# Offsets between the moving and the stationary tiles of TensorE, set stage by stage

## The chip, the cores and the metric

The kernel runs on one core of a Trainium2 chip. The time is that of one execution on the device, in microseconds. Besides plain timed runs there is one profiled execution, whose trace is read here: it lists each instruction of TensorE (PE, with its weight loads as PEld), VectorE (DVE), ScalarE (ACT), GpSimd (POOL) and the DMA queues with start and end.

## The reference

A small network on 256 tokens of width 1024, all in float32. The first block is stick-breaking attention, a squared-ReLU MLP, retention and a second MLP. The second block is a hybrid mixer (gated delta rule and forgetting attention beside each other), then a layer of 16384 experts from which each head picks 16 by product keys:

```python
for layer in range(DEPTH):                       # first_block
    hn = rms_norm(h, g_mix[layer])
    h = h + (stick_breaking_attention(...) if layer % 2 == 0 else retention(...))
    h = h + squared_relu_mlp(rms_norm(h, g_mlp[layer]), w_mlp_up[layer], w_mlp_down[layer])
...
res = res + hybrid_mixer(rms_norm_2(res, norm_mix), ...)      # second_block
# peer_ffn: scores, top-k, softmax gate, then
act = gelu(einsum('thkd,td->thk', expert_u[idx], xb))
out = einsum('thk,thkd->td', gate_w * act, expert_v[idx])
```

## The kernel before

All products with weights are made in three passes of the format fp32r: each float32 operand is split into a high part and the rest (ScalarE copies the high part, VectorE subtracts: lines 277 and 278 for weights, 150 and 151 for activations), and `mm3` (lines 84 to 91) issues high by high (L88), high by rest (L89), rest by high (L91). Each of these matmuls has a stationary operand of 128 columns, which a LDWEIGHTS brings into the array, and a moving operand of 256 columns that streams through it. While one matmul streams, the weights of the next one are loaded. So two operands are read from SBUF at the same time: the moving tile of this matmul and the stationary tile of the next.

Weights come through `Weights`: SP's queue loads a raw tile of 128x1024 floats some tiles ahead (line 247), and the split halves stand in tiles `whi` and `wlo` of fixed size, so that their start within a partition, counted modulo 512 bytes, is the same for all. Activations (`nh`/`nl` before a layer, `uh`/`ul` in the MLP, `yh`/`yl` before an output projection, `br..` in the hybrid's branches) stand in tiles whose rows are 1024 bytes long. Where they start is set by small unused tiles that `shift(pool, n)` allocates ahead of them (n bytes, lines 153 to 155), and, for `nh`/`nl`, by the argument of `norm_begin` (an offset in bytes within a larger tile, lines 158 to 168). Where the weights are the moving operand (token-major projections `pv`, list `moving` of `weight_plan`), `split` places them at an offset within a larger tile (line 251, in elements).

The stages, in order, with the name of the PSUM tile of each product: attention (`pq`, `pk`, `pv`, `pout`, until about 125 us of the profile), MLP 0 (`pu` up, `pd` down, until 300), retention (`pqk`, `pv`, `pg`, `pout`, until 497), MLP 1 (`pu` until 585, `pd` until 675), the hybrid (until 1034, with its output branches `py` and `pout` until 1101), and the expert layer `peer`: queries `pq`, top-16 choice on VectorE and the experts' up products `ph` beside each other (until 1323), the table of gates G built with float32 matmuls `pg` between `ph` products (until 1582), and the down products `acc`. In those the weights are the moving operand, 512 columns wide, and the stationary operand is a 128-column piece of `ch` or `cl`, the split product of activation and gate (lines 1586 to 1599). The loads of the next weights and of the spilled activations run beside this on the DMA queues.

In the built program before, the start of the moving tile minus the start of the stationary tile that is loaded beside it is 192 modulo 512 bytes in every one of these stages, except in the hybrid's input projections, where the rows of the moving tile are 1088 bytes long, so that the distance takes all multiples of 64 in turn (and, for the 260 columns of its `pq`, 48 more than these).

Of the kernel before, what the change touches and what calls it, by code (L numbers as in the profile page):

```python
# [9 lines left out]
F32R = mybir.dt.float32r  # L10
# [8 lines left out]
T = 256  # L19
# [202 lines left out]
class Weights:  # L222
# [18 lines left out]
    def prefetch(self, i, raws=None, parts=None):  # L241

        raws = min(i + 2 * self.bufs if raws is None else raws, len(self.plan))
        parts = min(i + self.bufs if parts is None else parts, len(self.plan))
        while len(self.raw) < raws:
            raw = self.wp.tile([128, 1024], F32, tag="raw", name="raw", bufs=self.bufs + 1)
            self.nc.sync.dma_start(raw, self.plan[len(self.raw)])
            self.raw.append(raw)
        while len(self.parts) < parts:
            i = len(self.parts)  # L250
            self.parts.append(self.split(self.raw[i], 96 if i in self.moving else 0))

    def first_half(self, i):

# [32 lines left out]
def sb_layer(k, h, next_gain):  # L287

    nc, a = k.nc, k.a
    x = (klist(k.nh), klist(k.nl))  # L290
    st = {}
    with k.tc.tile_pool(name="sb", bufs=2) as sp:
# [91 lines left out]
        def main():  # L384
            yield from project_qk(0)
            for g in range(1, 4):
                yield from project_qk(g)
                yield from project_v(g - 1)
            yield from project_v(3)
            k.norm_begin(256)  # L390

            for b in (0, 2):
                ps = [k.lin([128, 2, T], "pout") for _ in range(2)]
                for i in range(2):
                    for j in range(2):
                        yield from k.proj_half(ps[j], a["w_sb_out"][b + j][i], i, xo)
                        yield
                for j in range(2):
                    m = 2 * (b + j)
                    nc.vector.tensor_tensor(h[:, m:m + 2, :], ps[j], h[:, m:m + 2, :], op=OP.add)  # L400
                    for i in range(2):
                        k.norm_tile(h, m + i, next_gain)
# [18 lines left out]
def mlp_layer(k, h, layer, after):  # L421
    nc, a = k.nc, k.a
    x = (klist(k.nh), klist(k.nl))
    with k.tc.tile_pool(name="mlp", bufs=2) as mp:
        k.shift(mp, 96 if layer else 192)
        uh = mp.tile([128, 32, T], F32R, name="uh", bufs=1)
        ul = mp.tile([128, 32, T], F32R, name="ul", bufs=1)
        for b in range(16):
            p = k.proj(a["w_mlp_up"][16 * layer + b], x, "pu")
            r = mp.tile([128, 2, T], F32, name="r")  # L430
            nc.scalar.activation(r, p, AF.Relu)
            sq = mp.tile([128, 2, T], F32, name="usq")
            nc.scalar.activation(sq, r, AF.Square)
            k.split(uh[:, 2 * b:2 * b + 2, :], ul[:, 2 * b:2 * b + 2, :], sq)
            if b == 0:
                rs = k.rstd_bc(k.ssq, T, "rstd")
                r2 = mp.tile([128, T], F32, name="rstd2", bufs=1)
                nc.vector.tensor_tensor(r2, rs, rs, op=OP.mult)
        xu = (klist(uh), klist(ul))
        after("begin")  # L440
        for m in range(8):
            p = k.proj_deep([a["w_mlp_down"][(8 * layer + m) * 4 + i] for i in range(4)], xu, "pd")
            d = mp.tile([128, T], F32, name="d")
            nc.vector.tensor_tensor(d, p, r2, op=OP.mult)
            nc.vector.tensor_tensor(h[:, m, :], d, h[:, m, :], op=OP.add)
            after(m)


def ret_layer(k, h, next_gain):
    nc, a = k.nc, k.a  # L450
    x = (klist(k.nh), klist(k.nl))
    with k.tc.tile_pool(name="ret", bufs=2) as rp:
        k.shift(rp, 192)
        yh = rp.tile([128, 16, T], F32R, name="yh", bufs=1)
        yl = rp.tile([128, 16, T], F32R, name="yl", bufs=1)
        cs = rp.tile([128, 2, T], F32, name="cs", bufs=1)
# [3 lines left out]
        r = None  # L460
        for hd in range(4):
            rot = []
            for i in range(2):
                p = k.proj(a["w_ret_in"][4 * i + hd], x, "pqk")
# [18 lines left out]
            for b in range(2):  # L483
# [10 lines left out]
                p = drain(steps)  # L494
# [32 lines left out]
            for b in range(2):  # L527
# [1 line left out]
                nc.vector.tensor_tensor(yy, yy, gts[b], op=OP.mult)  # L529
                t0 = 4 * hd + 2 * b  # L530
                k.split(yh[:, t0:t0 + 2, :], yl[:, t0:t0 + 2, :], yy)
        k.norm_begin(256)
        xy = (klist(yh), klist(yl))
        for m in range(8):
            p = k.proj_deep([a["w_ret_out"][2 * m + i] for i in range(2)], xy, "pout")
# [13 lines left out]
class Hybrid:  # L549
# [749 lines left out]
    def branches(self, next_gain, get_ready):  # L1299

        k, nc, a = self.k, self.k.nc, self.k.a
        with k.tc.tile_pool(name="hbr", bufs=2) as bp:
            k.shift(bp, 96)

            xn = (klist(k.nh), klist(k.nl))
            yh = bp.tile([128, 8, T], F32R, name="yh", bufs=1)
            yl = bp.tile([128, 8, T], F32R, name="yl", bufs=1)
            gates = {bi: bp.tile([128, 2, T], F32, name=f"gate{n}", bufs=1) for n, bi in enumerate(gate_order()[:6])}
            pieces = {i: [tuple(bp.tile([128, T], F32R, name=f"br{z}{i}{m}", bufs=1) for m in range(8)) for z in "hl"]
                      for i in range(2)}  # L1310
            for n, bi in enumerate(gate_order()):
                if n < 6:
                    nc.scalar.dma_start(gates[bi], self.spill[n])
                else:
                    gates[bi] = bp.tile([128, 2, T], F32, name=f"gate{n}", bufs=1)

            def parts(i):
                for m in range(8):
                    k.split(pieces[i][0][m], pieces[i][1][m], (self.ob if i else self.oa)[:, m, :])
                return pieces[i]  # L1320

            for b, i in gate_order()[6:]:
                self.gate(gates[b, i], k.proj(a["w_hyb"][28 + 4 * i + b], xn, "pg"))
            x = {}
            for b in range(4):
                for i in (1, 0):
                    gt = gates[b, i]
                    if i not in x:
                        x[i] = parts(i)
                    p = k.proj(a["w_branch"][4 * i + b], x[i], "py")  # L1330
                    nc.vector.scalar_tensor_tensor(gt, gt, 1.0, p, op0=OP.add, op1=OP.mult)
                y = gates[b, 1]
                nc.vector.tensor_tensor(y, y, gates[b, 0], op=OP.add)
                hi = yh[:, 2 * b:2 * b + 2, :]
                nc.scalar.activation(hi, y, AF.Copy, scale=0.5)
                nc.vector.scalar_tensor_tensor(yl[:, 2 * b:2 * b + 2, :], y, 0.5, hi.bitcast(F32), op0=OP.mult,
                                               op1=OP.subtract)
            get_ready()
            xy = (klist(yh), klist(yl))
            for b in range(4):  # L1340
                p = k.proj(a["w_hyb_out"][b], xy, "pout")
                if b:
                    k.ahead.prefetch(0, parts=b - 1)
                hh = self.h[:, 2 * b:2 * b + 2, :]
                nc.vector.tensor_tensor(hh, p, hh, op=OP.add)
                for m in range(2):
                    k.norm_tile(self.h, 2 * b + m, next_gain)
# [33 lines left out]
def peer(k, h, gi, scoring):  # L1381
# [3 lines left out]
    with ExitStack() as ctx:  # L1385
        pp = ctx.enter_context(tc.tile_pool(name="peer", bufs=1))
        up = ctx.enter_context(tc.tile_pool(name="up", bufs=2))
        k.shift(up, 320)
        dr = ctx.enter_context(tc.tile_pool(name="spill", bufs=1, space=bass.MemoryType.DRAM))
        cols = pp.tile([128, 3, T], F32, name="cols")  # L1390
        iota = pp.tile([128, 128], F32, name="iota")
        nc.gpsimd.iota(iota, pattern=[[1, 128]], base=0, channel_multiplier=0, allow_small_or_imprecise_dtypes=True)
        spill = dr.tile([64, 128, 2, T], F32, name="spill")
        nh, nl = k.nh, k.nl
        r = k.rstd_bc(k.ssq, T, "rstd", pool=pp)
        rc = k.col(r, "rcol")
        xh = k.operand(k.act, "nh", T, 256)
        xl = k.operand(k.act, "nl", T, 256)
        x = (klist(xh), klist(xl))

        def normed(i):
# [169 lines left out]
        with tc.tile_pool(name="ops", bufs=1, space=PSUM) as ops:  # L1571
# [8 lines left out]
            for n, j in enumerate(down_order()):  # L1580
# [4 lines left out]
                    nc.scalar.dma_start(act, spill[j // 2])  # L1585
                c = up.tile([128, 2, T], F32, tag="t1", name="c")
                nc.vector.tensor_tensor(c, act, G[:, j:j + 2, :], op=OP.mult)
                ch = up.tile([128, 2, T], F32R, tag="t2", name="ch")
                cl = up.tile([128, 2, T], F32R, tag="t3", name="cl")
                k.split(ch, cl, c)  # L1590
                ws = [k.load_w(a["expert_v"][j + i]) for i in range(2)] if n == 63 else None
                c0, c1 = ([[z[:, i, 128 * t:128 * t + 128] for t in range(2)] for i in range(2)] for z in (ch, cl))
# [60 lines left out]
def body(tc, a, stop=None, start=None):  # L1653
    nc = tc.nc
    with ExitStack() as ctx:
# [11 lines left out]
        def after_gain(gi):  # L1667
            def f(m):
                if m == "begin":
                    k.norm_begin(256)  # L1670
                else:
                    k.norm_tile(h, m, gi)
            return f
# [3 lines left out]
        def get_ready():  # L1677

            k.shift(ctx.enter_context(tc.tile_pool(name="end", bufs=1, side="right")), 32)
            k.ahead = Weights(tc, ctx, peer_plan(a), 2, halves=True, side="right", name="wpp")  # L1680
            k.ahead.prefetch(0, parts=0)
            k.shift(c2.enter_context(tc.tile_pool(name="gap", bufs=1, side="right")), 320)
            k.norm_begin(0, c2.enter_context(tc.tile_pool(name="pnorm", bufs=1, side="right")))

        if start == "peer":
# [4 lines left out]
        else:  # L1690
            with ExitStack() as c1:
                plan, moving = weight_plan(a)
                k.w = Weights(tc, c1, plan, 3, moving=moving)
                with tc.tile_pool(name="attp", bufs=1, space=PSUM) as k.attp:
                    k.norm_begin(256)
                    splits = []
                    for i in range(2):
                        load_stream((i,))
# [121 lines left out]
```

## Time and profile before

| | us |
|---|---|
| median of 3 runs | 1948.25 (1946.83 to 1958.43) |
| profiled execution, its own time | 1947.31 |
| its span, first to last instruction | 1945.6 |
| PE busy / DVE busy / ACT busy | 1924.5 / 1426.5 / 1119.8 |

Of the profiled execution 1.7 us lie outside the span. A matmul's record lasts longer than the step from one matmul's start to the next, because matmuls are pipelined. What a stretch costs is therefore its length divided by the matmuls that start in it, and not the mean duration of one.

### The profile page before, as it was taken

How to read it: one execution, taken by the hardware profiler on the slowest of the kernel's cores; microseconds unless marked ns; L12 is line 12 of the kernel's file. 1: busy time of each engine (PE TensorE's matmuls, PEld its weight loads, DVE VectorE, ACT ScalarE, POOL GpSimd, SP SyncE). 2: the span in 40 equal slices, each digit the busy share in tenths (PEclk: the TensorE clock that was granted, in tenths of full speed). 3: DMA queues.
4: the chain of work that ended last, by engine and by line, in shares of the span. 5: the costliest groups of instructions: out<-in, count | busy, mean ns of one | idle time of the engine just before them, and what ended most of it. 6: DMA issues, size and time to landing. Idle time of an engine off the chain costs nothing.

```text
span 1945.6 us, 38035 instructions
## 1 busy us (share of the span) xinstructions
PE 1924.5 (99%) x14787; PEld 1819.0 (93%) x14787; DVE 1426.5 (73%) x2840; ACT 1119.8 (58%) x1761; POOL 118.7 (6%) x187
## 2 busy tenths in 40 slices
PE   8999999999999999999999999999999999999999
PEld 7999999999999988999899999999999998888887
DVE  5575556766655598688776799998888867777775
ACT  7776545556664475545555565446666655555554
POOL 2110000000000100110100111110000000000000
PEclk9999999999999999999999999999999999999999
DMA  6456666555666553332256357776555567777775
GB/s 196 141 164 194 196 195 191 166 177 174 207 192 192 174 168 98 98 99 77 88 188 219 125 179 226 222 226 189 179 179 176 180 206 235 235 236 234 236 234 179
DMA packets 109413, 353.63 MB, mean 182 GB/s; under 512 B 12832, under 2 KB 15664, under 8 KB 109104
## 3 DMA queue, kind: packets, MB, share of 16 engines
q1 hardware_dynamic: 97104, 329.82, 54.1%
q10 hardware_dynamic: 12128, 21.38, 3.4%
q8 instruction: 116, 1.90, 0.4%
q14 instruction: 65, 0.53, 0.1%
HBM read 332.28 MB, written 18.87 MB: 180 GB/s over the span
## 4 chain that ended last, share of the span: by engine, by line
PE 90%; DVE 6%; issue 3%; ACT 1%; POOL 0%; DMA 0%; SPq 0%; DVEq 0%; POOLq 0%; ACTq 0%
PE acc L1597 6%; PE acc L1596 6%; PE acc L1599 6%; PE ph L91 6%; PE ph L88 6%; PE ph L89 6%; PE pd L88 3%; PE pd L91 3%; PE pd L89 3%; PE pu L89 3%; PE pg L1565 3%; PE pu L91 3%; PE pu L88 3%; DVE wlo L278 2%; PE pv L88 1%
## 5 line engine op out<-in xcount | busy, mean ns | idle before, releaser
L278 DVE TENSOR_TENSOR wlo<-raw,whi 128x512 fp32r<-128x512 f32 (+1 forms) x863 | 774.4, 901 | 341.9 <-ACT whi L277 291.8
L277 ACT ACTIVATE whi<-raw 128x512 fp32r<-128x512 f32 (+1 forms) x863 | 675.1, 788 | 601.4 <-PE acc L1597 158.0
L88 PE MATMUL ph<-nh,whi 128*128 128x256 f32 x1024 | 258.7, 287 | 0.2 <-ACT whi L277 0.2
L89 PE MATMUL ph<-nl,whi 128*128 128x256 f32 x1024 | 253.0, 281 | 0.0
L1596 PE MATMUL acc<-whi,ch 128*128 128x512 f32 x504 | 198.7, 394 | 0.0
L1597 PE MATMUL acc<-whi,cl 128*128 128x512 f32 x504 | 198.6, 394 | 0.0
L88 PEld LDWEIGHTS ph<-nh,whi 128*128 128x128 f32 x1024 | 194.1, 190 | 0.4 <-ACT whi L277 0.4
L89 PEld LDWEIGHTS ph<-nl,whi 128*128 128x128 f32 x1024 | 194.1, 190 | 0.0
L91 PE MATMUL ph<-nh,wlo 128*128 128x256 f32 x1024 | 163.7, 282 | 0.9 <-DVE wlo L278 0.8
L1599 PE MATMUL acc<-wlo,ch 128*128 128x512 f32 x504 | 158.0, 394 | 0.0
L91 PEld LDWEIGHTS ph<-nh,wlo 128*128 128x128 f32 x1024 | 139.6, 190 | 1.8 <-DVE wlo L278 1.7
L89 PE MATMUL pu<-nl,whi 128*128 128x256 f32 x512 | 122.9, 277 | 0.3 <-DVE nl L183 0.3
L88 PE MATMUL pu<-nh,whi 128*128 128x256 f32 x512 | 123.0, 277 | 0.0
L88 PE MATMUL pd<-uh,whi 128*128 128x256 f32 x512 | 121.5, 279 | 0.0
L89 PE MATMUL pd<-ul,whi 128*128 128x256 f32 x512 | 121.4, 278 | 0.0
L1596 PEld LDWEIGHTS acc<-whi,ch 128*128 128x128 f32 x504 | 94.3, 187 | 23.4
L1597 PEld LDWEIGHTS acc<-whi,cl 128*128 128x128 f32 x504 | 94.3, 187 | 23.3
L1599 PEld LDWEIGHTS acc<-wlo,ch 128*128 128x128 f32 x504 | 94.2, 187 | 23.3
L89 PEld LDWEIGHTS pu<-nl,whi 128*128 128x128 f32 x512 | 96.1, 188 | 0.7 <-DVE nl L183 0.5
L88 PEld LDWEIGHTS pd<-uh,whi 128*128 128x128 f32 x512 | 96.5, 189 | 0.0
L89 PEld LDWEIGHTS pd<-ul,whi 128*128 128x128 f32 x512 | 96.5, 189 | 0.0
L88 PEld LDWEIGHTS pu<-nh,whi 128*128 128x128 f32 x512 | 96.2, 188 | 0.1
(553 smaller groups left out, 4218.9 us busy)
## 6 DMA issues: line engine op xcount, KB each, us to landing
raw<-expert_u SPq DMA_DIRECT2D x128, 512.0 KB, 3.8
raw<-expert_v SPq DMA_DIRECT2D x128, 512.0 KB, 4.3
raw<-w_hyb SPq DMA_DIRECT2D x72, 512.0 KB, 3.5
raw<-w_mlp_up SPq DMA_DIRECT2D x64, 512.0 KB, 4.3
raw<-w_mlp_down SPq DMA_DIRECT2D x64, 512.0 KB, 3.9
raw<-w_ret_in SPq DMA_DIRECT2D x48, 512.0 KB, 3.8
spill<-act SPq DMA_DIRECT2D x62, 256.0 KB, 2.7
act<-spill ACTq DMA_DIRECT2D x62, 256.0 KB, 3.6
```

The source lines that it names most:

```text
L88: mm(out, wh[k], xh[k], start=first and k == 0, stop=False, skip_group_check=True)
L89: mm(out, wh[k], xl[k], start=False, stop=False, skip_group_check=True)
L91: mm(out, wl[k], xh[k], start=False, stop=last and k == n - 1, skip_group_check=True)
L277: nc.scalar.activation(hi, src, AF.Copy)
L278: self.last = nc.vector.tensor_tensor(lo, src, hi.bitcast(F32), op=OP.subtract).ins
L1565: nc.tensor.matmul(pg[:, i, :], A[:, i, :], B[:, i, :], start=True, stop=True)
L1596: mm(acc[t][d], c0[i][t], vh, start=False, stop=False, skip_group_check=True)
L1597: mm(acc[t][d], c1[i][t], vh, start=False, stop=False, skip_group_check=True)
L1599: mm(acc[t][d], c0[i][t], vl, start=False, stop=False, skip_group_check=True)
```

## The change

Only sizes of unused tiles and offsets within tiles change; one tile moves to another pool, and `ch` and `cl` become views of tiles with 64 more columns.

```diff
-            self.parts.append(self.split(self.raw[i], 96 if i in self.moving else 0))
+            self.parts.append(self.split(self.raw[i], 64 if i in self.moving else 0))
...
-            k.norm_begin(256)
+            k.norm_begin(288)
...
-        k.shift(mp, 96 if layer else 192)
+        k.shift(mp, 128 if layer else 160)
...
-        k.shift(rp, 192)
+        k.shift(rp, 96)
...
-        k.norm_begin(256)
+        k.norm_begin(240)
...
-            k.shift(bp, 96)
+            k.shift(bp, 448)
...
-        k.shift(up, 320)
+        k.shift(up, 384)
...
-        r = k.rstd_bc(k.ssq, T, "rstd", pool=pp)
+        r = k.rstd_bc(k.ssq, T, "rstd")
...
-        xh = k.operand(k.act, "nh", T, 256)
-        xl = k.operand(k.act, "nl", T, 256)
+        xh = k.operand(k.act, "nh", T, 288)
+        xl = k.operand(k.act, "nl", T, 288)
...
-                ch = up.tile([128, 2, T], F32R, tag="t2", name="ch")
-                cl = up.tile([128, 2, T], F32R, tag="t3", name="cl")
+
+                ch, cl = (up.tile([128, 2 * T + 64], F32R, tag=x, name=f"c{x}")[:, 0:2 * T]
+                          .rearrange("p (i t) -> p i t", i=2) for x in ("t2", "t3"))
...
-                    k.norm_begin(256)
+                    k.norm_begin(272)
...
-            k.shift(c2.enter_context(tc.tile_pool(name="gap", bufs=1, side="right")), 320)
+            k.shift(c2.enter_context(tc.tile_pool(name="gap", bufs=1, side="right")), 416)
...
-                    k.norm_begin(256)
+                    k.norm_begin(96)
```

What this does to the distance (start of the moving tile minus start of the stationary tile loaded beside it, modulo 512 bytes), from the addresses of the two built programs, with the number of matmuls of each product:

| product | matmuls | before | after |
|---|---|---|---|
| attention `pq`, `pk` | 384 | 192 | 32 |
| attention `pv` | 192 | 192 | 224 |
| attention `pout` | 192 | 192 | 192 |
| MLP 0 `pu` | 768 | 192 | 224 |
| MLP 0 `pd` | 768 | 192 | 160 |
| retention `pqk`, `pg` | 768 | 192 | 208 |
| retention `pv` | 384 | 192 | 48 |
| retention `pout` | 384 | 192 | 96 |
| MLP 1 `pu` | 768 | 192 | 176 |
| MLP 1 `pd` | 768 | 192 | 224 |
| hybrid input projections | 1728 | all multiples of 64, and 48 more | the same |
| hybrid `py`, `pout` | 576 | 192 | 32 |
| experts `pq` | 384 | 192 | 96 |
| experts `ph` | 3072 | 192 | 224 |
| experts `acc` (512 wide) | 1536 | 192 | 128 and 384, by turns |

So 9216 matmuls with 256 moving columns get a distance that is no multiple of 64 bytes, and the 1536 of `acc` one that still is. Every engine has the same instructions in the same order as before; the one difference is that a wait of TensorE on eight DMA semaphores, which stood before the two transposes of `rstd` (line 216) at the start of the expert layer, stands before its first matmul with the keys instead.

## Rows read from the trace of the kernel before

**Rows 1.** The page, part 1: engine, busy us (share), instructions.
```profile
span 1945.6 us, 38035 instructions
...
PE 1924.5 (99%) x14787; PEld 1819.0 (93%) x14787; DVE 1426.5 (73%) x2840; ACT 1119.8 (58%) x1761; POOL 118.7 (6%) x187
```

**Rows 2.** Busy time of each engine by stage (the second line names the columns).
```profile
core 0: us, PE busy (x) PEld busy (x) DVE busy (x) ACT busy (x) POOL busy (x), PEclk, DMA share, GB/s
...
213.00:300.00 87.00, 87.00 (x770) 87.00 (x770) 50.26 (x54) 40.86 (x50) 6.15 (x6) 1.00 0.64 195
...
675.00:1034.00 359.00, 355.20 (x2920) 330.61 (x2919) 281.81 (x751) 199.62 (x389) 27.82 (x58) 1.00 0.38 121
...
1101.00:1152.00 51.00, 51.00 (x440) 50.95 (x439) 47.51 (x151) 33.19 (x66) 7.51 (x10) 1.00 0.53 166
1152.00:1323.00 171.00, 169.49 (x1432) 168.08 (x1431) 167.72 (x530) 86.99 (x151) 30.01 (x40) 1.00 0.72 223
1323.00:1560.00 237.00, 234.71 (x2004) 234.46 (x2005) 194.54 (x460) 157.09 (x226) 0.42 (x1) 0.99 0.55 178
1582.00:1946.00 364.00, 359.99 (x1551) 288.48 (x1549) 251.36 (x381) 193.25 (x319) 0.00 (x0) 1.00 0.73 227
```

**Rows 3.** TensorE alone in stretches inside stages: (x) counts its matmuls.
```profile
220.00:295.00 75.00, 75.00 (x665) 1.00 0.64 196
465.00:495.00 30.00, 30.00 (x257) 1.00 0.64 187
505.00:583.00 78.00, 78.00 (x691) 1.00 0.64 193
590.00:665.00 75.00, 75.00 (x639) 1.00 0.62 186
1036.00:1076.00 40.00, 40.00 (x356) 1.00 0.59 196
1160.00:1235.00 75.00, 75.00 (x639) 1.00 0.71 225
1600.00:1900.00 300.00, 300.00 (x1287) 1.00 0.76 234
```

**Rows 4.** Groups on PE, 213 to 300 us: busy us, mean ns of one.
```profile
L89 PE MATMUL pd<-ul,whi 128*128 128x256 f32 x256 | 59.6, 276 | 0.0
```

**Rows 5.** The same groups, 585 to 675 us.
```profile
L89 PE MATMUL pd<-ul,whi 128*128 128x256 f32 x256 | 61.7, 281 | 0.0
```

**Rows 6.** Timeline on PE, start and us, where one stage follows another.
```profile
584.36 0.28 PE L89 MATMUL pu<-nl,whi 128*128 128x256 f32 x1
...
584.47 0.62 PE L91 MATMUL pu<-nh,wlo 128*128 128x256 f32 x4
...
584.93 0.29 PE L568 MATMUL psm<-rmeta,ones 128*128 128x16 f32 x2
...
585.07 0.36 PE L88 MATMUL pd<-uh,whi 128*128 128x256 f32 x1
...
585.27 0.28 PE L89 MATMUL pd<-ul,whi 128*128 128x256 f32 x1
...
585.38 0.28 PE L88 MATMUL pd<-uh,whi 128*128 128x256 f32 x1
```

**Rows 7.** Groups on PE in the hybrid stage, 676 to 1034 us.
```profile
L89 PE MATMUL pg<-nl,whi 128*128 128x256 f32 x128 | 31.7, 281 | 0.0
...
L89 PE MATMUL pq<-nl,whi 128*128 128x260 f32 x64 | 16.6, 288 | 0.0
...
L89 PE MATMUL pqb<-nl,whi 128*128 128x256 f32 x64 | 16.0, 282 | 0.0
```

**Rows 8.** Groups on PE in the retention stage, 300 to 450 us.
```profile
L89 PE MATMUL pv<-wlo,nh 128*128 128x256 f32 x128 | 31.3, 279 | 0.0
...
L89 PE MATMUL pqk<-nl,whi 128*128 128x256 f32 x128 | 30.7, 277 | 0.0
```

**Rows 9.** Groups on PE in the gate table stage, 1330 to 1555 us.
```profile
L89 PE MATMUL ph<-nl,whi 128*128 128x256 f32 x481 | 119.3, 282 | 0.0
```

**Rows 10.** Groups in the last stage, 1600 to 1900 us.
```profile
L1596 PE MATMUL acc<-whi,ch 128*128 128x512 f32 x429 | 169.0, 394 | 0.0
...
L278 DVE TENSOR_TENSOR wlo<-raw,whi 128x512 fp32r<-128x512 f32 x214 | 147.8, 690 | 85.2 <-ACT whi L277 85.1
```

## Prediction

> **What bounds the kernel now.** I read the page's first part, then the busy time by stage, then TensorE alone in stretches that lie inside one stage. The first shows PE busy in 1924.5 of 1945.6 us, so there is hardly an idle gap to win [rows 1]; what can change is the step from one matmul to the next. That step is read from [rows 3]: the length of a stretch, divided by its matmuls less two (those that started before its edge). [...] The steps fall on two values. The MLP 0 down product takes 75.00/663 = 113.1 ns, MLP 1 up 78.00/689 = 113.2, the hybrid's `py` 40.00/354 = 113.0. MLP 1 down takes 75.00/637 = 117.7, retention `pout` 30.00/255 = 117.6, `ph` 75.00/637 = 117.7. All of these have the same shape (128x256), and the same distance of 192. The two MLP downs are the same code: 276 ns for one matmul in the first [rows 4], 281 in the second [rows 5]. So there are two modes, a short step and a long one, and in the long one a matmul costs 117.7 - 113.1 = 4.6 ns more. The last stage, `acc`, has 512 columns and takes 300/1285 = 233.5 ns, more than two short steps of 256 (226.2).
>
> How a mode is entered can be seen where MLP 1 down begins [rows 6]: up to there the steps are 0.11 us, a small matmul (`psm`, 16 columns) comes between, the first `pd` follows late, and from there the long step holds for the whole stage. Nothing on another engine ends a wait there. I read this as two streams, the moving tile and the next weights, that disturb each other or not depending on how they meet. The distance between their addresses is one part of that, and the moment of the last break in the stream another. In the hybrid's projections, where the distance runs through all multiples of 64, the 256-column products show 281 and 282 ns, and never 276 [rows 7]: there the long step is the rule. That is the best sign in this trace that distance counts; that 192 shows both modes is the sign that it isn't all.
>
> **The change part by part.** No instruction is added, removed or moved, so every term is a number of matmuls by a step. I take for the forecast that the new distances bring the short step of 113.1 ns to nearly all 256-column products.
>
> - MLP 1 down: 768 matmuls, all at the long step: 768 x 4.6 ns = 3.5 us.
> - Retention `pout`: 384 x 4.6 = 1.8 us.
> - `ph` beside the gate table, 1330 to 1555 us: three groups of 480 or 481 at 281 to 292 ns [rows 9], so 1442 at the long step, and some 190 up to 1582: 1630 x 4.6 = 7.5 us. PE is busy in 234.71 of 237.00 us there and DVE in 194.54 [rows 2], so DVE has room to follow.
> - `pq` and `ph` beside the top-16 choice, 1101 to 1323 us: some 1800 matmuls, most at the long step, 7 us by count. But DVE is busy in 47.51 + 167.72 = 215.2 of 222 us there [rows 2]. It makes the low halves of the weights in the same queue as the choice, so PE would soon wait for those. At most 6.8 us can go; I take 2.
> - Attention, retention projections, the hybrid's outputs: mixtures. In retention, `pv` has 279 ns and `pqk` 277 [rows 8], between 276 and 281, so a fifth to three fifths have the long step. With some 840 of them (an estimate from such means) it is 4 us.
> - `acc`: 1536 matmuls. [...] I take twice the short 256-column step, 226.2: 7.3 x 1536 = 11 us. DVE, at 251.36 of 364 us [rows 2], has its longest wait on ACT, and its 690 ns for a split leave it room [rows 10].
> - A loss: some 4000 matmuls have the short step now (all of MLP 0, MLP 1 up, `py`, parts of others), and one that falls to the long step loses 4.6 ns, 18 us for all. I take a fifth: 4 us.
> - The moved wait before the expert layer: DMAs of a stage long past; nothing. If they were late, the first matmul with the keys would wait in place of the transposes, a few matmuls later. The larger `ch`/`cl` tiles cost no instruction.
>
> Sum: 3.5 + 1.8 + 7.5 + 2 + 4 + 11 - 4 = 26 us. The profiled execution took 1947.3 us, so 1921.3; it lies 0.9 us under the median of 1948.25, which makes 1922.
>
> [...]
>
> **The rivals.**
>
> *No effect.* The mode is set by the moment of the last break in the stream, not by the distance: 192 gives both. The same breaks would then leave the same modes, and the time is 1948, give or take 8. [...] Against it: the means of the hybrid's products, where the distance varies, hold no short step at all [rows 7].
>
> *Part of it.* The plain stages get the short step, `acc` nothing: its distances of 128 and 384 are multiples of 64 still. The sum is then 26 - 11 = 15 us, so 1933.
>
> *Slower.* Moving tiles that start off the 64-byte grid cost more in themselves. The only products of before with such a distance are those of `pq` with 260 columns: 288 ns, where the 256-column `pqb` of the same stage has 282 [rows 7]. [...] It decides from the point where the step in MLP 0 is above 115.4 ns, half way between the modes. Against it: in those rows the distance changes with every second matmul, and in the new stages it is constant.
>
> *Much faster.* The short step is not the floor either. [...] For it: nothing in the rows, none has a step below 113.0. [...]
>
> **How the numbers follow.** Chances: forecast (1922) 0.40, part of it (1933) 0.17, no effect (1948) 0.20, slower 0.13, much faster 0.10. One per cent of the median, 19.5 us, is about what a measurement of this kernel tells from no change. The forecast lies 26 us below, and six sevenths of its own spread (1905 to 1935) are beyond 1%; with much faster and a third of the partial case that makes 0.50 for faster. Slower by over 1% is most of the slower rival and a little of no effect, 0.13; within 1%, 0.37. The range leaves out half of much faster and the dear half of slower: 1888 to 1962.
>
> **What would show it.** In the profile after, MLP 1 down should take 87 us and not 90, with 276 ns for one; `ph` beside the gate table 276 ns and 5 to 8 us less; `acc` a step near 226 ns or below, and its stage some 353 us instead of 364. From 1101 to 1323 little should go, with new waits of `ph` on `wlo`. MLP 0 should stay at 113 ns. The forecast is wrong if `ph` and MLP 1 down keep 117.7 (no effect), if `acc` keeps 233.5 (part of it), or if MLP 0 and `py` lose their 113 (slower).

## The result, and the profile after

The changed kernel takes 1964.70 us (median of 15 runs, 1964.34 to 1967.45), the kernel before 1953.72 in 15 runs beside it (1944.67 to 1958.43). The ratio, taken from all the runs, is 1.0068 [1.0055, 1.0081]: slower by 0.7% (the two medians alone give 0.6%). The forecast was 1922, 26 us faster, and the range ended at 1962. One more thing stands out: the runs before spread over 14 us, in two clumps (six from 1944.67 to 1948.93, nine from 1953.27 to 1958.43), those after over 3.

The profiled execution took 1964.51 us. The page's part 1, engine, busy us (share), instructions, for comparison with [rows 1]:

```profile
span 1962.8 us, 38034 instructions
...
PE 1943.6 (99%) x14787; PEld 1842.7 (94%) x14787; DVE 1427.8 (73%) x2840; ACT 1122.9 (57%) x1761; POOL 116.9 (6%) x187
```

The span grew by 17.2 us and PE's busy time by 19.1. DVE and ACT did the same work in nearly the same time (1427.8 and 1122.9 us, where it was 1426.5 and 1119.8), and PE has as little idle time as before (19 us, and 21). So the step from one matmul to the next grew. Here is TensorE alone in stretches inside stages of the kernel after, read as [rows 3]: MLP 0 up and down, retention `pout`, MLP 1 up and down, `py`, experts' `pq`, `ph`, `acc`.

```profile
core 0: us, PE busy (x), PEclk, DMA share, GB/s
...
130.00:210.00 80.00, 80.00 (x674) 1.00 0.62 185
225.00:300.00 75.00, 75.00 (x642) 1.00 0.61 188
...
465.00:505.00 40.00, 40.00 (x334) 1.00 0.62 183
515.00:595.00 80.00, 80.00 (x671) 1.00 0.61 190
610.00:685.00 75.00, 75.00 (x637) 1.00 0.61 187
1055.00:1092.00 37.00, 37.00 (x319) 1.00 0.63 196
1125.00:1160.00 35.00, 35.00 (x297) 1.00 0.45 151
1180.00:1255.00 75.00, 75.00 (x636) 1.00 0.70 223
1620.00:1900.00 280.00, 280.00 (x1207) 1.00 0.75 236
```

By the same reckoning (length over matmuls less two) MLP 0 down is 75.00/640 = 117.2 ns where it was 113.1; MLP 1 up is 80.00/669 = 119.6 where it was 113.2; retention `pout` 40.00/332 = 120.5 where it was 117.6; MLP 1 down 75.00/635 = 118.1 where it was 117.7. The granted clock is 1.00 in all. `acc` went from 233.5 to 280.00/1205 = 232.4. The mean length of one matmul says the same of the 256-column products, less sharply; of `acc` it doesn't (395 ns against 394, though the step fell), so the step is what counts. Groups on PE (the tile name `ct` stands for `ch` and `cl` here), 126 to 217 us, 218 to 307, and the last stage, against 276 ns in [rows 4] and 394 in [rows 10]:

```profile
L89 PE MATMUL pu<-nl,whi 128*128 128x256 f32 x254 | 63.3, 281 | 0.1
...
L89 PE MATMUL pd<-ul,whi 128*128 128x256 f32 x255 | 61.3, 280 | 0.0
...
L1597 PE MATMUL acc<-whi,ct 128*128 128x512 f32 x402 | 158.6, 395 | 0.0
```

The starts of the stages, each taken from its first matmul in the two traces, show where the 17 us came from. From here on "step" is the mean time from one matmul's start to the next within a product, without the gaps where PE waited; it differs from the reckoning from stretches by up to 0.7 ns, either way.

| | start before | start after | later by | step before | step after |
|---|---|---|---|---|---|
| MLP 0 up | 125.0 | 126.2 | 1.2 | 113.4 | 118.3 |
| MLP 0 down | 213.4 | 218.0 | 4.6 | 113.3 | 117.3 |
| retention projections (`pqk`) | 300.4 | 308.1 | 7.7 | 113.8 | 119.1 |
| retention `pout` | 451.5 | 463.1 | 11.6 | 117.2 | 120.0 |
| MLP 1 up | 497.2 | 509.3 | 12.1 | 113.6 | 119.3 |
| MLP 1 down | 585.1 | 601.5 | 16.4 | 117.8 | 118.3 |
| hybrid `py` | 1034.3 | 1051.1 | 16.8 | 113.4 | 116.7 |
| experts `pq` | 1100.6 | 1118.6 | 18.0 | 116.9 | 119.9 |
| experts `ph` | 1152.5 | 1171.5 | 19.0 | 117.5 | 118.3 |
| `acc` | 1583.3 | 1602.0 | 18.7 | 233.3 | 232.4 |
| last matmul of `acc` | 1941.6 | 1958.8 | 17.2 | | |

The loss is made in MLP 0 (6.5 us), the retention projections (3.9) and MLP 1 up (4.3). These had the short step of 113 ns for the most part (in retention `pqk` 113.8, `pg` 114.6), and at the new distances nothing has it any more.

### The profile page after: what moved, and what is told of

It reads as the page before. It is cut to its first block, busy times and chain, and to the rows that moved or that the text cites. A ratio compares the mean times of both kernels' runs of the same rounds, so it can differ in the third digit from the quotient of the medians.

```text
span 1962.8 us, 38034 instructions
## 1 busy us (share of the span) xinstructions
PE 1943.6 (99%) x14787; PEld 1842.7 (94%) x14787; DVE 1427.8 (73%) x2840; ACT 1122.9 (57%) x1761; POOL 116.9 (6%) x187
## 4 chain that ended last, share of the span: by engine, by line
PE 90%; DVE 5%; issue 2%; DMA 1%; ACT 1%; POOL 0%; SPq 0%; DVEq 0%; POOLq 0%; ACTq 0%
PE acc L1597 6%; PE acc L1600 6%; PE acc L1598 6%; PE ph L88 6%; PE ph L89 6%; PE ph L91 6%; PE pd L89 3%; PE pd L91 3%; PE pd L88 3%; PE pu L89 3%; PE pu L91 3%; PE pu L88 3%; PE pg L1565 3%; DVE wlo L278 2%; PE pout L88 2%
## 5 line engine op out<-in xcount | busy, mean ns | idle before, releaser
L89 PE MATMUL ph<-nl,whi 128*128 128x256 f32 x1024 | 253.8, 281 | 0.0
L1597 PE MATMUL acc<-whi,ct 128*128 128x512 f32 x504 | 198.9, 395 | 0.0
L1598 PE MATMUL acc<-whi,ct 128*128 128x512 f32 x504 | 198.8, 394 | 0.0
L89 PEld LDWEIGHTS ph<-nl,whi 128*128 128x128 f32 x1024 | 193.0, 188 | 0.0
L1600 PE MATMUL acc<-wlo,ct 128*128 128x512 f32 x504 | 158.0, 395 | 0.0
L89 PE MATMUL pu<-nl,whi 128*128 128x256 f32 x512 | 127.7, 282 | 0.1
L88 PE MATMUL pu<-nh,whi 128*128 128x256 f32 x512 | 127.6, 282 | 0.0
L89 PE MATMUL pd<-ul,whi 128*128 128x256 f32 x512 | 123.5, 281 | 0.0
L1600 PEld LDWEIGHTS acc<-wlo,ct 128*128 128x128 f32 x504 | 95.0, 188 | 22.2
L1597 PEld LDWEIGHTS acc<-whi,ct 128*128 128x128 f32 x504 | 95.0, 188 | 22.1
L1598 PEld LDWEIGHTS acc<-whi,ct 128*128 128x128 f32 x504 | 95.0, 188 | 22.1
L89 PEld LDWEIGHTS pu<-nl,whi 128*128 128x128 f32 x512 | 96.6, 189 | 0.4 <-DVE nl L183 0.3
L89 PEld LDWEIGHTS pd<-ul,whi 128*128 128x128 f32 x512 | 96.2, 188 | 0.0
```

Of the source, the lines that this page charges most:

```text
L88: mm(out, wh[k], xh[k], start=first and k == 0, stop=False, skip_group_check=True)
L89: mm(out, wh[k], xl[k], start=False, stop=False, skip_group_check=True)
L1597: mm(acc[t][d], c0[i][t], vh, start=False, stop=False, skip_group_check=True)
L1598: mm(acc[t][d], c1[i][t], vh, start=False, stop=False, skip_group_check=True)
L1600: mm(acc[t][d], c0[i][t], vl, start=False, stop=False, skip_group_check=True)
```

## Experiments

**The same kernel once more.** The prediction left open whether the moment of the last break in the stream sets the mode (theory M in the expectations) or the distance. So first nothing was changed.

> The kernel before once more, profiled again. Theory D (the distance decides alone): at 192 each stage keeps the step that it had, MLP 0 113 ns, MLP 1 down 117.7, py 113. Theory M (at 192 the moment of the last break in the stream decides between two steps): some stage changes its step from this profile to the last, MLP 1 down or a pout at 113 or MLP 0 at 118, with no instruction changed, and the time moves with it by 3 to 4 us for each MLP half.

Measured: 1946.82 us. Most stages repeated their step, but some changed it without any change of an instruction: attention `pout` 114.7 to 117.8 ns, the hybrid's `pout` 116.8 to 113.4, `ph` 117.5 to 115.9. TensorE alone in the hybrid's `pout`, first in this run, then in the run of [rows 3], has five matmuls more in the same 18 us:

```profile
1080.00:1098.00 18.00, 18.00 (x157) 1.00 0.20 68
```

```profile
1080.00:1098.00 18.00, 18.00 (x152) 1.00 0.20 64
```

At distance 192 there are two modes, then, and the same instructions get now one and now the other. In `ph` of this run both stand within one stage: some 1170 of its steps are of 113 or 114 ns and some 1470 of 117 to 119. No MLP half changed between these two runs, and both were short ones (1947.31 and 1946.82 us), so they don't show by themselves where the 14 us of spread come from; the run of `acc` by itself, further down, bears on that.

**The change in two parts.** Only `acc` (before, with the wider tiles):

```diff
-        k.shift(up, 320)
+        k.shift(up, 384)
...
-                ch = up.tile([128, 2, T], F32R, tag="t2", name="ch")
-                cl = up.tile([128, 2, T], F32R, tag="t3", name="cl")
+                ch, cl = (up.tile([128, 2 * T + 64], F32R, tag=x, name=f"c{x}")[:, 0:2 * T]
```

> The kernel before with the edits on the down products alone (wider ch and cl, shift of 384 in place of 320, rstd in the other pool), so distances of 128 and 384 for acc and 192 elsewhere. If my sum for acc was right the step falls from 233.5 to 226 ns and the time by 11 us; if acc is indifferent, as its stage of 357 against 358 us in the changed kernel says, the time is that of before within 2 us.

Everything but `acc` (after, with these lines as before):

> The changed kernel with the edits on the down products undone: acc back at 192, all other distances new. If the loss comes from the 256-column products, 1962 to 1968, as the changed kernel. If the acc edits carry part of it, some 1955.

Measured: `acc` alone 1948.48 us, ratio 0.9984 [0.9965, 1.0003]; its step 232.4, so 0.9 ns by 1536 matmuls = 1.4 us. Without it 1966.90, ratio 1.0080 [1.0057, 1.0103], with all the 256-column steps of the table (`acc` 233.3). The whole loss is that of the 256-column products.

**Both tiles off the 64-byte grid, the distance kept.** The rival "slower" held that a start off that grid costs in itself (theory S). Here weights and activations both start 32 bytes later, and the distance remains 192.

```diff
+        if moving:
+            self.wp.tile([128, 8], F32, name="wshift", bufs=1)
...
-            k.norm_begin(256)
+            k.norm_begin(288)
...
-        k.shift(up, 320)
+        k.shift(up, 288)
```

> The kernel before with both tiles moved by 32 bytes: moving and stationary tiles start off the 64-byte grid, the distance stays 192 in all stages but the hybrid's input projections. Theory D or M (the distance to the other tile matters): MLP 0 keeps 113 ns and the time is that of before, 1945 to 1958. Rival S (the start of a tile off the 64-byte grid costs in itself): steps of 117 to 120 ns in MLP 0, MLP 1 up and py, and 1962 or more. The hybrid's input projections, whose distances leave the grid here, stay at 118 to 119 ns by either.

Measured: 1947.09 us, ratio 0.9967 [0.9948, 0.9986]. TensorE alone in MLP 0 up and down, MLP 1 up and down of this kernel:

```profile
130.00:210.00 80.00, 80.00 (x680) 1.00 0.62 187
225.00:300.00 75.00, 75.00 (x639) 1.00 0.61 188
505.00:580.00 75.00, 75.00 (x662) 1.00 0.67 202
590.00:665.00 75.00, 75.00 (x664) 1.00 0.62 194
```

These are 118.0 and 117.7 ns, then 113.6 and 113.3: the same two values as at distance 192 on the grid, in other stages. MLP 0 did not keep its 113 ns, as D and M had it, but MLP 1 and `py` (113.4) have the short step with both tiles off the grid, and MLP 0 has the long step on the grid too in two kernels further down (the break moved, `acc` by itself). So a start 32 bytes off the grid costs nothing by itself; S falls for such a start. (The kernels at 180 below show another start that does count.)

**One distance for the whole kernel.** The next four kernels set the distance to 0, 64, 128 and 448 in every product outside the hybrid's input projections, `acc` included, by the same arguments (at 0: `shift` 512, `norm_begin` 64). One theory (P) had the step repeat after 256 bytes, so that 448 acts as 192; another (G) had every multiple of 64 act alike.

> The kernel before with a distance of 0 modulo 512 in every stage in place of 192 (acc too). Theory G (any multiple of 64 bytes allows the short step, what is between does not): steps of 113 or 118 ns stage by stage, by the breaks, and 1940 to 1958. Theory P (192 is a place of its own, with a period of 256 or 512 bytes): no stage at 113, all at 117 to 120, and 1962 or more.

> The same with a distance of 64. Theory G: steps of 113 or 118 ns, 1940 to 1958. Theory P: no stage at 113, 1962 or more; the hybrid rows of before at 64 and 0 (281 to 282 ns for one) lean to that.

> The same with a distance of 128. Theory G: steps of 113 or 118 ns, 1940 to 1958. Theory P: no stage at 113, 1962 or more.

> The same with a distance of 448, that is 192 and 256. Theory G: steps of 113 or 118 ns, 1940 to 1958. Theory P with a period of 256: the same as at 192, 1944 to 1958 with some stages at 113; with a period of 512: no stage at 113 and 1962 or more.

| distance | time, us | 256-column products, ns | `acc`, ns |
|---|---|---|---|
| 0 | 1969.58 | 119.4 to 120.0 | 226.7 |
| 64 | 1959.10 | 117.0 to 117.9, attention `pv` 114.8 | 228.9 |
| 128 | 1969.19 | 118.5 to 119.4 | 232.4 |
| 448 | 1953.74 | 113.3 (`py`) to 117.8 | 233.3 |

Each is one run, and the kernel before took 1948.54 beside them. TensorE alone at distance 0, MLP 0 up and `acc`:

```profile
130.00:210.00 80.00, 80.00 (x665) 1.00 0.58 181
...
1620.00:1900.00 280.00, 280.00 (x1237) 1.00 0.79 241
```

80.00/663 = 120.7 and 280.00/1235 = 226.7: the worst of these four for 256 columns is the best for 512. 448 shows the pair of steps of 192. G falls at 0 and 128, and so does "no effect": with the same instructions, the distance alone took every stage that it was set in off the short step. P stands at 0, 128 and 448. At 64 it missed: the time is under 1962, and `pv` has both steps there (47 of its matmuls, from 38.68 to 43.89 us, start 113.3 ns apart, others 117.8), so 64 can give the short step too, in a product whose moving operand is the weights.

**The distance stepped within a stage.** The weights are put later by 16 bytes more after every four tiles in MLP 0, by 4 bytes more in MLP 1, and `ch`/`cl` by 16 bytes more in `acc`, so that some 96 matmuls of one run share each distance. In MLP 1 the moving tile stands 32 bytes off the 64-byte grid in this kernel.

```diff
-            self.parts.append(self.split(self.raw[i], 96 if i in self.moving else 0))
+            self.parts.append(self.split(self.raw[i], 96 if i in self.moving else self.off(i)))
...
+        return 4 * ((i - 32) // 4) if 32 <= i < 96 else (i - 160) // 4 if 160 <= i < 224 else 0
```

> The kernel before with the distance stepped within stages: in MLP 0 from 192 down in steps of 16 bytes every 96 matmuls (the split weights start 16 bytes later each time), in MLP 1 from 224 down to 164 in steps of 4 bytes, in the down products of the experts from 192 down in steps of 16 bytes every 96 matmuls. Theory F (the step is a function of the distance modulo 256, with two values at 192 alone): the values of the whole-stage runs come back, 117.8 at 64, 120.0 at 0 and 96, 118.7 at 128, 116.7 at 32 and 48, 119.2 at 176 and 208; acc 233.3 at 192, 232.4 at 128, 228.9 at 64, 226.7 at 0, and the rest is new. Rival H (the stage and its neighbours make the step, the distance only at 192): no pattern that agrees with them.

Measured, step in ns by distance modulo 256:

```
MLP 0: 192 117.3, 176 118.8, 160 118.7, 144 119.9, 128 120.0, 112 118.3, 96 119.9, 80 118.1, 64 117.8,
       48 116.7, 32 116.7, 16 119.9, 0 120.0, 240 118.3, 224 118.4, 208 117.8
MLP 1: 224 118.3, 220 119.9, 216 119.2, 212 117.8, 208 117.8, 204 113.6, 200 117.8, 196 119.6,
       192 113.5, 188 118.4, 184 118.3, 180 113.4, 176 118.8, 172 120.0, 168 113.6, 164 118.2
acc:   240, 0 and 16 226.7 to 226.9, 64 228.9, 80 230.0, 176 232.0, 160 234.3, others 233.3
```

TensorE alone at distance 208, 204, 200, then 184, 180, 172, 168, each over 10.5 us of its stretch:

```profile
551.00:561.50 10.50, 10.50 (x92) 1.00 0.67 199
562.20:572.70 10.50, 10.50 (x95) 1.00 0.69 201
573.10:583.60 10.50, 10.50 (x92) 1.00 0.63 197
618.40:628.90 10.50, 10.50 (x91) 1.00 0.61 199
629.70:640.20 10.50, 10.50 (x95) 1.00 0.58 197
652.00:662.50 10.50, 10.50 (x90) 1.00 0.60 196
663.50:674.00 10.50, 10.50 (x95) 1.00 0.64 197
```

95 matmuls against 90 to 92. Four distances have the short step: 204, 192, 180, 168, twelve bytes apart. None of the sixteen in MLP 0 has it; 192 ran in the other of its two modes there. This answers to the kernel after: 224 gave 118.3 there and 118.3 here, 32 116.7 and 116.7, 96 120.0 and 119.9, 176 119.3 and 118.8, although there the moving tile was shifted and here the weights. So H falls, and F holds for most values. The distance is nearly the whole story but not all of it: 208 gave 119.1 after and 117.8 here (in both MLPs), 160 117.3 after and 118.7 here, 128 118.7 in its own kernel and 120.0 here (`acc` 232.4 and 233.3).

**The break moved.** To see whether the small `psm` matmul sets MLP 1 down's mode [rows 6], it was put behind the first `pd` product (the kernel before else).

```diff
-        after("begin")
...
+            if m == 1:
+                after("begin")
+                after(0)
```

> The kernel before with what follows MLP 1 up (the small matmul psm above all) done after the first of the eight down products in place of before them; the distances stay at 192. Theory M: the first 96 matmuls of MLP 1 down go on at the step that MLP 1 up ended with (113.3 where it had that), and only the break by psm sets a new one, 113.3 or 117.8, for the other 672. Rival: the stage's tiles set the step; then it is 117.8 from its first matmul on.

Measured: 1954.07 us, MLP 1 down 117.8 as in the kernel before. But MLP 1 up ran at 117.5 already in this run, so there was no short step for the break to end. Inconclusive.

**`acc` by itself.** The kernel before with `acc` at distance 0, one number changed:

```diff
-        k.shift(up, 320)
+        k.shift(up, 512)
```

> The kernel before with one number changed, the shift ahead of ch and cl (512 in place of 320), so that acc has a distance of 0 and all else 192. Theory F: acc falls from 233.3 to 226.7 ns, 1536 x 6.6 = 10 us, so some 1942 against 1952 of before, ratio 0.995. Rival: the gain of u0 in that stage came with its other distances (less in front of it to wait for); then no change.

Measured: 1933.03 us (7 runs), ratio 0.9912 [0.9894, 0.9930]; step 226.7, the stage 348 us and not 358. That is the prediction's term for `acc`, which it had at the wrong distance. The medians differ by more than these 10 us; in the traces `ph`, still at 192, took 4 us less too, with a step of 115.1 between the two modes.

The trace shows something else. MLP 0 up and down, with nothing changed in them, have 680 and 640 matmuls where the run of [rows 3] has 706 (130 to 210 us) and 665:

```profile
130.00:210.00 80.00, 80.00 (x680) 1.00 0.61 187
220.00:295.00 75.00, 75.00 (x640) 1.00 0.61 190
```

Both halves ran in the long step, and MLP 0 took 6.4 us more than in the kernel before, MLP 1 up, at 117.5, 2.9 us more. (In the run with the break moved these three stages had the long step as well.) Such changes of mode are of the size that parts the two clumps of the kernel before, whose medians lie 7 us apart; that they make the clumps is likely but not shown, since no run of the upper clump was traced.

All 64 multiples of 4 bytes, 24 matmuls each (before, with `[:, n:n + 2 * T]` for `ch` and `cl`):

> The kernel before with the distance of the down products stepped through all 64 multiples of 4 bytes modulo 256, one per step of two experts (24 matmuls each), by starting ch and cl later within wider tiles; the moving tile (the weights) stays where it is. If 226.7 ns (twice 113.3) is the least that 512 columns take, no distance has less, and several have 226.7, among them 240, 0 and 16. If the short step of the 256-column products at 180 and 204 has its like here, some distance has 220 ns.

Measured: no step under 226.7, which was reached near 0 (at 4, 28, 52) and at 112; the rest lies between 227 and 237. 16 gave 228.3 here and 226.9 in the first sweep, 240 233.2 and 226.7, 112 226.7 and 233.3. So few matmuls at each distance don't settle a value.

**Weights twelve bytes off.** Three kernels hold the distance at 180, 168 or 204 (460 modulo 512) by shifting the weights, with `acc` at 0. For `pv` and `ph`, where the weights move or stand in other tiles, the moving tile is shifted instead.

```diff
-            self.parts.append(self.split(self.raw[i], 96 if i in self.moving else 0))
+            self.parts.append(self.split(self.raw[i], 93 if i in self.moving else 3 if self.moving else 0))
...
-        xh = k.operand(k.act, "nh", T, 256)
+        xh = k.operand(k.act, "nh", T, 244)
```

> acc at 0 as in the run before, and all other stages at 180 in place of 192 (weights 12 bytes later; ph by its own tile; the experts' pq stays at 192; the hybrid's input projections move by 12 bytes too). Theory K (one look at 180 within a stage had 113.4 ns straight after a stretch at the long step, so at 180 the short step is entered without fail): 113 to 114 ns in every stage, also beside the gate table, and some 1920 to 1928. Rival L (180 is like 192, two steps, and the break decides): a mixture of 113.3 and 117.8 by stage, 1931 to 1941 as with acc at 0 alone.

> The same with 168 (24 bytes later). Theory K: 113 to 114 ns in every stage, 1920 to 1928. Rival L: a mixture, 1931 to 1941.

> The same with 204 modulo 256 (12 bytes earlier). Theory K: 113 to 114 ns in every stage, 1920 to 1928. Rival L: a mixture, 1931 to 1941.

| distance | time, us | ratio | both MLPs, ns | `pv` | `ph` |
|---|---|---|---|---|---|
| 180 | 1936.77 | 0.9929 [0.9904, 0.9954] | 113.3 to 113.4 | 120.2 | 120.3 |
| 168 | 1951.41 | 1.0002 [0.9985, 1.0019] | 119.6 to 120.0, MLP 1 down 113.3 | 120.4 to 120.5 | 120.5 |
| 204 | 1933.08 | 0.9913 [0.9883, 0.9944] | 113.3 to 113.4 | 118.1 to 119.1 | 118.0 |

At 180 and 204 the short step came to every MLP stage, retention `pout` and `py`. 168 has it in MLP 1 down, retention `pout` and `py` (113.3 to 113.6), but not in MLP 0 and MLP 1 up, against what the sweep's 96 matmuls had said. K fails at all three: no time is within its 1920 to 1928, and `pv` and `ph` never have the short step. In those the same 180 gives 120 with the moving tile shifted. The line of `ph` on PE at 180, 1330 to 1550 us, against 282 ns in [rows 9]:

```profile
L89 PE MATMUL ph<-nl,whi 128*128 128x256 f32 x466 | 117.4, 283 | 0.0
```

So which tile starts where counts too. It is not on or off the 64-byte grid alone: in the sweep's MLP 1 the moving tile was 32 bytes off, and 180 had 113.4 ns.

**All of it together.** The last kernel puts only stationary weights twelve bytes later and leaves moving tiles on the grid; both halves of a weight share one tile, two small tiles go elsewhere to make room, and `acc` has 0 and 256.

```diff
-            self.parts.append(self.split(self.raw[i], 96 if i in self.moving else 0))
+            self.parts.append(self.split(self.raw[i], 32 if i in self.moving else 3 if self.moving or i < 144 else 0))
...
-        k.shift(up, 320)
+        k.shift(up, 256)
```

> Distance 180 modulo 256 wherever the stationary tile is a weight (ph and pq included), by starting the split weights 12 bytes later and leaving the moving tile on the 64-byte grid; pv stays at 192, acc at 0. To make room the two halves of an expert's weights share a tile, and a small mask moves into the attention's pool. Theory N (the short step is certain when the moving tile starts on the grid and the stationary one 12 bytes off it; v180 lost it in pv and ph, where the moving tile was off): 113.3 ns in ph too, where v180 had 120.3, and some 1920 to 1926. Rival E (the expert stage differs, whatever the starts): ph at 117 to 120 and 1930 to 1937.

Measured: 1924.91 us (1924.62 to 1925.28), ratio 0.9855 [0.9839, 0.9871]; it beats both kernels. TensorE alone in both MLPs (up, down, `pout` of retention between them), `py` and `acc`; then groups on PE from 1330 to 1550 us, for comparison with [rows 9] (L86 is their L89):

```profile
130.00:210.00 80.00, 80.00 (x707) 1.00 0.65 193
225.00:295.00 70.00, 70.00 (x620) 1.00 0.66 193
465.00:495.00 30.00, 30.00 (x267) 1.00 0.65 197
505.00:580.00 75.00, 75.00 (x664) 1.00 0.66 198
590.00:660.00 70.00, 70.00 (x620) 1.00 0.65 195
1033.00:1073.00 40.00, 40.00 (x355) 1.00 0.64 200
...
1580.00:1880.00 300.00, 300.00 (x1325) 1.00 0.75 242
```

```profile
L86 PE MATMUL ph<-nl,whi 128*128 128x256 f32 x485 | 116.5, 276 | 0.0
```

All are 113.2 to 113.5 ns, `acc` is 226.8, and `ph` has 276 ns where it had 282 (its step is 113.9): N stands, and E falls. `pv`, left at 192, has 117.2 and 117.8. Its four runs differ by 0.7 us, not 14, and the six at 180 above by 2.7: hardly any mode was left to chance at this distance in these runs.

## Why the prediction was wrong

- **The step that failed** is the one sentence on which the sum stood: "that the new distances bring the short step of 113.1 ns to nearly all 256-column products". The new distances are 32, 48, 96, 160, 176, 208 and 224, and each of them has 116.7 to 120.0. What failed is the inference from [rows 7]: products with changing distances showed the long step, and I read that as "distance counts", which is right, but not as "192 is one of the few good ones", which those very rows said too. With 0 and 128 at 118.5 to 120.0, and 64 at 117 to 118 outside attention `pv`, 192 was the one multiple of 64 (modulo 256) at which most products could have the short step.
- **MLP 1 down, retention `pout`, `ph`, the outputs** (3.5 + 1.8 + 9.5 + 4 us to gain): MLP 1 down lost 0.4 us, retention `pout` 0.5, `pq` 1.0, `py` 1.3; `ph` held its length (426.8 us against 427.3) at 118.3 ns. Where the short step did come, in the last kernel, MLP 1 down gained 3.4 us and retention `pout` 1.4, close to their terms; `ph` with `pq` gained 6.3 of 9.5 (`ph` takes 421.4 us there), and attention, the retention projections and the hybrid's `pout` together under 1 of 4. These two terms were too large even with the step granted. With `acc` the last kernel gained 22 us between the traced runs; that its time is near the forecast of 1922 is no sign for the forecast, which had it from other distances.
- **The loss** was put at a fifth of some 4000 matmuls, 4 us. All of those that had the short step lost it, 3.3 to 5.7 ns each: 6.5 + 4.3 + 3.9 + 1.3 = 16 us in MLP 0, MLP 1 up, the retention projections and `py`.
- **`acc`**: 11 us forecast, 1.4 measured alone. Twice the short step, 226.2, was the right aim (226.7 at 0, 10 us), but 128 and 384 don't reach it (232.4).
- **The moved wait** and the wider tiles: nothing, as said; the kernel with them and the distances of `acc` alone is no slower (1948.48 us, ratio 0.9984).
- **No effect** falls by the distances 0 and 128 (118.5 to 120.0 ns in the 256-column products that they were set in). It named a true thing, though, for 192: there a mode changes without the distance. But that the same breaks leave the same modes is not so: the mode changed from run to run with nothing changed (the hybrid's `pout` 116.8 and 113.4 ns). At one shape the step was 120.0 ns at 0 and 113.5 at 192 within one run, the sweep (mean granted clock 0.999). Weight loads and matmuls run at the same time (in the kernel after PEld is busy for 94% of the span and PE for 99%), but whether it is their two reads that disturb each other, as the prediction read it, no run shows.
- **Slower** had the sign and its point of decision (MLP 0 above 115.4: it has 117.3 and 118.3). The size, 17 us between the traces, is near the 18 us that the prediction's bullet on the loss has for all matmuls with the short step. Its cause was another for nearly all of the loss: not the start off the grid in itself, since with both tiles 32 bytes off and the distance kept there are still 113.3 to 113.6 ns in MLP 1, but the distance, since the sweep has the steps of 224, 32 and 96 (118.4, 116.7 and 119.9 in MLP 0) again with the moving tile on the grid. A part of the rival lives on in `ph` at 180, where the moving tile's start does cost (120.3 ns against 113.9 in the last kernel). What its dear half, which the range leaves out, would cost, no run shows. The chance of 0.13 for it was too small, since [rows 7] spoke for it more than for the forecast.
- **Much faster** falls: in all the runs no 256-column product has a mean step under 113.3, and no `acc` one under 226.7. What a shorter step would bring, which stands behind the low end of the range, no run shows.
- **Against the median** the loss is 11 us and in the traces 17, because the profiled execution of before (1947.31) was one of its shorter ones. The forecast, too, started from a median of three, 1948.25, where fifteen gave 1953.72. A spread of 14 us in a kernel whose instructions never change was likely a sign of modes left to chance (the four runs of the last kernel differ by 0.7 us), and I took it for noise.

What stays open: why twelve bytes, why 168 holds in one stage and not in another, why 208, 160 and 128 have two values, and what picks the mode at 192.

## What to carry to other kernels

Where TensorE is busy throughout, read its step (stretch over matmuls) stage by stage and compare stages of one shape: here PE was idle in 21 of 1945.6 us, and what was left was a few ns on each of thousands of matmuls (113.3 against 117.8, and 226.7 against 233.3 in `acc`). If the same shape shows two steps, measure the placement of the moving tile against the stationary one by a sweep inside one run before choosing a value, for each width apart (0 had 120.0 ns at 256 columns and 226.7 at 512), and keep the one that gives the same step in every stage and every run. Rows that show a variable to matter don't show which value of it is good.

## What was not expected of the hardware

The step changes with 4 bytes of distance: 204 has 113.6 ns, 200 and 208 have 117.8 (one run, 96 matmuls each). The best distances for 256 columns (180 and 204, 113.3 to 113.4 ns in both MLPs) and for 512 (0, 226.7) differ, and 0 is among the worst for 256 (119.4 to 120.0) and among the best for 512. It counts which of the tiles is moved: 180 is 113.9 for `ph` with the weights off the grid, 120.3 with the moving tile. And four of the steps that whole stages hold, 113.3 and 120.0, 226.7 and 233.3, are whole multiples (17, 18, 34, 35) of 6.67 ns (120.0/18); others, above all the 117.8 of the long step, which is as steady, are not. That is an observation of these runs, with no cause shown.
